# Three token groups cut anew (512, 64 + 768, 768), six PSUM banks for the first one's blocks, and moved steps in a one-core decoder layer

## The chip, the cores and the metric

The kernel runs on one core of one Trainium2 chip. The metric is the device time in microseconds of one execution. Before the change the median of three runs is 2630.23 us (2629.91 to 2632.38).

## What is computed

One layer of a decoder for 2048 prompt tokens and 64 sample tokens (8 sequences of 8), 1024 wide, in float32. Both kinds of token use the same weights; each sample sequence starts from a state of its own.

```python
def mixer(h, pos, s_ret, s_hg, w_in, ret_norm_w, hgrn_norm_w, lb, w_out):
    proj = h @ w_in                       # 1024 x 4096: rq rk rv rg hq hf hi hg, 4 heads of 128 each
    ...
    o_r, s_ret_new = chunk_gla(rq, rk, rv, log_g_ret, s_ret)     # retention, a fixed decay per head
    o_r = head_rmsnorm(o_r, ret_norm_w) * silu(rg)
    f = lb_h + (1.0 - lb_h) * sigmoid(hf)
    o_h, s_hg_new = chunk_gla(silu(hq) * dk ** -0.5, 1.0 - f, hi, log(f), s_hg)
    o_h = head_rmsnorm(o_h, hgrn_norm_w) * silu(hg)
    return concatenate([o_r, o_h]) @ w_out, s_ret_new, s_hg_new

x = x + mixer(rmsnorm(x, norm_mix_w), ...)
x = x + square(relu(rmsnorm(x, norm_ffn_w) @ w_up)) @ w_down     # 1024 x 4096, 4096 x 1024
y = rmsnorm(x, final_norm_w)
```

`chunk_gla` is the recurrence S_t = diag(g_t) S_(t-1) + k_t v_t^T, o_t = S_t^T q_t. Outputs are y for both kinds of token and the last states of both recurrences.

## The kernel before

**Groups.** Tokens lie along the free dimension, 128 features on the partitions. They are worked in three groups (`GROUPS`, L37): 64 sample + 512 prompt tokens, then 768, then 768 prompt tokens. Each group goes through the whole layer before the next; the recurrent states `S` are handed on. A group's slab is one tile of 128 x 768 float32 (`SLAB`, L29); the pool `sl` holds 46 (`NSLAB`), and `get` (L227) takes one. A group's columns are cut into two pieces for PSUM: twice 288 in the first group, twice 384 in the others (L391).

**Three products for one.** Every weight and activation is split into a high part in float32r (a cast on ScalarE) and the rest, the lower half (a subtraction on VectorE or GpSimd). A product is high x high, high x low and low x high, all float32r matmuls. `proj` (L314) runs a projection like that into a tile `pj` of two PSUM banks, of which there are two; four more banks form the pool `pm` (`mm`, L346), which the mixing and the norms use. `weight` (L242) casts weight tiles of 128 x 1024 two ahead of use; three of four lower halves (L271) are GpSimd's, the fourth VectorE's.

**Order.** The order of work is written out by hand. Each three-way step of a projection ends with a `tick` (L211), a count, not a time. Steps are put on an agenda with `at` and `later`, so many ticks on, and are issued when the count gets there; `flush` (L220) issues all that is left at once. A tick is two matmuls of a group's two pieces, or three matmuls in the values (`values`, L672). A scheduler orders the instructions of each engine by priority and free buffers after that; `keep_in_program_order` pins some.

**Stages of a group.** `norm_in` (L494) loads, casts and squares the group's input, spread over the end of the group before it, and turns its sum of squares into a factor per token. `mix` (L578) runs four heads; each projects its gates, keys, queries and values and puts the steps of `mixer` (L758) on the agenda: logs and scans, then for six block widths the exponents on GpSimd (L792), the exponentials on ScalarE (L797), the decayed products on VectorE (L803) and their matmuls (`level`); the products of a token with itself (`own`, summed over the partitions at L470, with halves cut at L331); the keys turned; then chunk by chunk the outputs (L997, L999) and states (L1005, with S on VectorE at L1012). A group with sample tokens also loads, uses and updates their states (L716 to L741). `out_proj_first` or `out_proj` (L1125, L1277) projects back: three heads' worth, added at L1119, then the fourth's, added at L1133 or L1292.

**FFN.** The first group's FFN is plain: 32 blocks up (`up_first`), 64 blocks down (`down_first`), each evicted by VectorE or ScalarE (L1198 is the addition after a down block). The other two use a seven-product scheme on 2 x 2 blocks (`up`, `down`, matmuls at L1105), apart from the first eighth of up. It needs sums of weight blocks. These are made during the first group's output projection and FFN: `plan_sums` (L1244) puts 15 sets on the agenda, each with four loads and four stores of 512 KB on the SP queue and four sums on VectorE (L1256), one set in 100 ticks from tick 90 after the mixing on.

**Last norm.** `finish_first` (L1213) and `finish` (L1578) normalize a group's result during the next group's mixing: eight squares on ScalarE, added on GpSimd (L491, L1588) every 8 ticks, then a sum over partitions, a factor (`last_factor`, L1623), and eight steps on VectorE (L1232, L1605) every 6 or 12 ticks, each followed by a store of y on SP. The last group ends with `finish(g, (1,), 1)` and `finish_last`.

Of the kernel before, what the change touches and what calls it, by code (L numbers as in the profile page):

```python
# [9 lines left out]
F32 = mybir.dt.float32  # L10
# [5 lines left out]
P = 128  # L16
# [12 lines left out]
SLAB = 768  # L29
NSLAB = 46  # L30
# [6 lines left out]
GROUPS = ((NS, 0, 512), (0, 512, 768), (0, 1280, 768))  # L37
# [58 lines left out]

def constants():
# [27 lines left out]
    pos = np.concatenate([np.tile(PAST + np.arange(SLEN), NSEQ), np.arange(SEQ)]).astype(np.float32)  # L125
# [72 lines left out]
class Kernel:  # L198
# [115 lines left out]
    def proj(self, g, blocks, acts, pieces=None):  # L314
# [3 lines left out]
        pj = self.pj.tile([P, 2, 512], F32, tag="pj", name="pj")  # L318
# [10 lines left out]
    def cut(self, src, hi, lo, T):  # L329
        self.tc.keep_in_program_order(self.nc.scalar.copy(hi[:, :T], src[:, :T]))  # L330
        self.nc.vector.tensor_tensor(out=lo[:, :T], in0=src[:, :T], in1=hi.bitcast(F32)[:, :T], op=ALU.subtract)  # L331

    def v2(self, slab, g):
        return slab[:, :g.T].rearrange("p (h t) -> p h t", h=2)
# [14 lines left out]
    def build(self):  # L349
        nc, tc, I = self.nc, self.tc, self.I  # L350
        with ExitStack() as ctx:
# [11 lines left out]
            self.ordered = True  # L363
# [21 lines left out]
            for ns, p0, n in GROUPS:  # L385
# [5 lines left out]
                g.pieces = [(0, g.T // 2), (g.T // 2, g.T)]  # L391
# [67 lines left out]
    def parts(self, src, n):  # L459

        t = self.getr()
        hi, lo = t[:, :n], t[:, SLAB // 2:SLAB // 2 + n]
# [9 lines left out]
    def halves(self, g, src):  # L472
        T2 = g.T // 2
        return [self.parts(src[:, hf * T2:(hf + 1) * T2], T2) for hf in range(2)]

    def both_sums(self, g, parts):

        out = []
        for hi, lo in parts:
            ps = self.mm(g.T // 2)  # L480
# [13 lines left out]
    def norm_in(self, g, start=False):  # L494


        nc, T, T2 = self.nc, g.T, g.T // 2
# [27 lines left out]
        def factor():  # L525
            g.rs, ln = self.get(), self.get()
            for hf in range(2):
                sl = slice(hf * T2, (hf + 1) * T2)
                ps = self.mm(T2)
# [46 lines left out]
        self.later(t0 + 28, factor_t, 3)  # L576
# [181 lines left out]
    def mixer(self, g, p, b, t0):  # L758
# [260 lines left out]
        step, late, chunk, wait = 13, 24, 7, 14  # L1019
# [4 lines left out]
        at(28, own, 0)  # L1024
        at(30, own, 1)
# [20 lines left out]
        at(t + 8, end_decays)  # L1046
# [687 lines left out]
```

## Time and profile before

| | |
|---|---|
| median of three runs | 2630.23 us |
| the profiled execution, its own time | 2629.84 us |
| its span, first to last instruction | 2628.0 us |
| ScalarE (ACT), busy | 1234.5 us (47%) |
| GpSimd (POOL), busy | 1089.9 us (41%) |
| mean granted TensorE clock | 0.995 |
| moved by DMA | 365.81 MB, 139 GB/s in the mean |

The first group's mixing is in the first 320 us of the span, its FFN ends near 795 us; the second group's mixing lies around 795 to 1210 us, the last one's FFN ends with the span.

The profile is one execution. PE is TensorE's matmuls, PEld its weight loads, which overlap them; DVE is VectorE, SP the engine that issues the transfers. A row of a group of instructions has line, engine, operation, output<-inputs, shapes and count; behind the bar the busy time and the mean ns of one, then the engine's idle time just before them and what ended it. A row of waits has who waited for whom, the total in us, how many times, and the longest. A matmul's mean is its latency; matmuls are pipelined, so the distance between two is shorter.

### The profile page before, as it was taken

To read this page: it belongs to the slowest core of one execution; us is meant where nothing else is said; L and a number is where in the kernel's file an instruction comes from. 1 tells how busy PE (TensorE), PEld (TensorE's weight loads), DVE (VectorE), ACT (ScalarE), POOL (GpSimd) and SP (SyncE) were. 2 spreads that over 40 slices of the span, in tenths; PEclk is the share of its full clock that TensorE was granted. 3 is DMA by queue.
4 is the path that set the end of the run, shared out by engine and by line. 5 is a ranking of instruction groups with operands and counts; after the bars stand their busy time and mean duration, and the time that the engine had idled before them with its cause. 6 is when DMAs were issued, how large, how long until landed. Compare 5 with 4: busy or idle time off the path is not lost. (4 is left out here: it accounts for less than half of the span.)

```text
span 2628.0 us, 41634 instructions
## 1 busy us (share of the span) xinstructions
PE 2570.6 (98%) x16999; PEld 2536.8 (97%) x16999; DVE 1683.9 (64%) x2077; ACT 1234.5 (47%) x1653; POOL 1089.9 (41%) x605
## 2 busy tenths in 40 slices
PE   8999999999999999999999999999999999999997
PEld 8999999999999999999999999989999999999997
DVE  6666776545565466565554988675665665549886
ACT  6555442222244555554543545455555445345443
POOL 6555557444436355431222332463554302223322
PEclk9999999999999999999999999999999999999999
DMA  5233366666752111122556755421111225566552
GB/s 181 81 97 90 121 217 241 232 252 221 266 183 85 57 49 49 53 66 69 166 174 203 261 169 199 145 97 49 46 44 59 70 69 178 179 207 209 175 178 81
DMA packets 125951, 365.81 MB, mean 139 GB/s; under 512 B 12480, under 2 KB 33984, under 8 KB 125760
## 3 DMA queue, kind: packets, MB, share of 16 engines
q1 hardware_dynamic: 125616, 363.13, 41.7%
q8 instruction: 134, 2.20, 0.3%
q14 instruction: 57, 0.47, 0.1%
q10 hardware_dynamic: 144, 0.02, 0.0%
HBM read 293.10 MB, written 69.99 MB: 138 GB/s over the span
## 5 line engine op out<-in xcount | busy, mean ns | idle before, releaser
L271 POOL TENSOR_TENSOR lo<-raw,hi 128x1024 fp32r<-128x1024 f32 x227 | 591.3, 2605 | 1257.6 <-ACT hi L256 1140.6
L323 PE MATMUL pj<-slab,hi 128*128 128x288 f32 (+1 forms) x5120 | 1016.8, 316 | 18.9 <-ACT hi L256 6.3
L323 PEld LDWEIGHTS pj<-slab,hi 128*128 128x128 f32 x5120 | 811.8, 189 | 25.2 <-ACT hi L256 9.3
L256 ACT CAST hi<-raw 128x1024 fp32r<-128x1024 f32 x402 | 422.3, 1052 | 847.1 <-PE pj L323 373.3
L323 PE MATMUL pj<-slab,lo 128*128 128x288 f32 (+1 forms) x2560 | 600.1, 315 | 1.8 <-POOL lo L271 1.7
L1105 PE MATMUL pd<-slab,hi 128*128 128x384 f32 x1792 | 457.2, 335 | 6.7 <-DVE slab L1551 3.1
L323 PEld LDWEIGHTS pj<-slab,lo 128*128 128x128 f32 x2560 | 430.0, 189 | 2.9 <-POOL lo L271 2.0
L1105 PE MATMUL pu<-slab,hi 128*128 128x384 f32 x1600 | 396.2, 334 | 0.0
L1105 PEld LDWEIGHTS pd<-slab,hi 128*128 128x128 f32 x1792 | 324.3, 188 | 8.4 <-DVE slab L1551 3.7
L271 DVE TENSOR_TENSOR lo<-raw,hi 128x1024 fp32r<-128x1024 f32 x175 | 231.6, 1323 | 156.0 <-ACT hi L256 152.7
L1105 PE MATMUL pd<-slab,lo 128*128 128x384 f32 x896 | 300.2, 335 | 0.9 <-POOL lo L271 0.9
L1105 PEld LDWEIGHTS pu<-slab,hi 128*128 128x128 f32 x1600 | 288.2, 188 | 0.0
L1105 PE MATMUL pu<-slab,lo 128*128 128x384 f32 x800 | 256.9, 334 | 0.0
L687 PE MATMUL pjv<-hi,slab 128*128 128x256 f32 x1088 | 211.6, 288 | 3.9 <-DVE slab L667 3.9
L1307 DVE TENSOR_TENSOR slab<-slab 128x768 fp32r<-128x768 f32 x144 | 162.3, 1143 | 41.4 <-ACT slab L1303 29.1
L687 PEld LDWEIGHTS pjv<-hi,slab 128*128 128x128 f32 x1088 | 175.5, 193 | 5.6 <-DVE slab L667 4.3
L1105 PEld LDWEIGHTS pd<-slab,lo 128*128 128x128 f32 x896 | 168.8, 188 | 1.5 <-POOL lo L271 1.5
L1303 ACT CAST slab<-slab 128x768 fp32r<-128x768 f32 x144 | 117.9, 833 | 108.3 <-DVE slab L1314 84.9
L687 PE MATMUL pjv<-lo,slab 128*128 128x256 f32 x544 | 155.0, 285 | 0.0
L1105 PEld LDWEIGHTS pu<-slab,lo 128*128 128x128 f32 x800 | 149.3, 188 | 0.0
L1521 DVE TENSOR_TENSOR slab<-pd,slab 128x768 f32<-128x768 f32 x110 | 104.1, 950 | 40.0 <-PE pd L1105 39.7
L797 ACT ACTIVATE slab<-slab 128x768 f32<-128x768 f32 (+2 forms) x72 | 56.3, 781 | 135.8 <-POOL slab L793 135.7
(197 smaller groups left out, 3405.2 us busy)
## 6 DMA issues: line engine op xcount, KB each, us to landing
raw<-w SPq DMA_DIRECT2D x342, 512.0 KB, 3.9
u<-ld SPq DMA_DIRECT2D x64, 384.0 KB, 4.6
slab<-u SPq DMA_DIRECT2D x64, 384.0 KB, 5.8
ld<-x SPq DMA_DIRECT2D x32, 384.0 KB, 4.6
y<-slab SPq DMA_DIRECT2D x12, 384.0 KB, 2.5
raw<-su1S SPq DMA_DIRECT2D x8, 512.0 KB, 3.7
raw<-su2S SPq DMA_DIRECT2D x8, 512.0 KB, 3.9
raw<-su3S SPq DMA_DIRECT2D x8, 512.0 KB, 4.0
```

Source lines behind the costliest of these rows:

```text
L256: self.nc.scalar.copy(hi, raw)
L271: eng.tensor_tensor(out=lo, in0=self.second.pop(j), in1=hi.bitcast(F32), op=ALU.subtract)
L323: self.nc.tensor.matmul(pj[:, i, :T2], w, a[:, c0:c1], start=j == 0 and q == 0, stop=j == n - 1 and q == 2)
L687: nc.tensor.matmul(pj[:, i * 256:(i + 1) * 256], a[:, s:s + C], ww, start=kb == 0 and q == 0, stop=kb == KB - 1 and q == 2)
L797: nc.scalar.activation(x["dd", w][:, a:T], x["dd", w][:, a:T], AF.Exp)
L1105: self.nc.tensor.matmul(*a, **k)
L1303: self.nc.scalar.copy(hi[:, :g.T], B[name][:, :g.T])
L1307: self.nc.vector.tensor_tensor(out=lo[:, :g.T], in0=B[name][:, :g.T], in1=hi.bitcast(F32)[:, :g.T], op=ALU.subtract)
L1521: nc.vector.tensor_tensor(out=r, in0=ps, in1=r, op=ALU.add)
```

## The change

What it does, by place:

- Groups are now 512 prompt tokens, 64 sample + 768 prompt tokens, 768 prompt tokens. The first group's columns are one piece of 512; the second's are two of 416. Slabs are 832 wide and 42 in number. Inputs, positions and outputs are laid out to match.
- From the first group's output projection to the end of its FFN (`spread`), two of three projections go to one bank of `pm`, the third to a `pj` tile.
- `plan_sums` runs ahead of the first mixing, one set in 148 ticks from tick 150 on.
- In `mixer`, the own sums come 4 ticks later, the exponentials and what follows them 2 ticks later; the second half of `cut` is issued 4 or 3 ticks after the first.
- In `out_proj_first` the lower halves come after 7 ticks instead of 4 and the flush at the end is gone; in `out_proj` they come 2 ticks later.
- The last norm's squares are added on VectorE, every 4 ticks; the output steps come every 5; the factor's last product is issued 4 ticks after what it needs. The last group's end keeps its pace and GpSimd.

```diff
-SLAB = 768
-NSLAB = 46
+SLAB = 832
+NSLAB = 42
...
-GROUPS = ((NS, 0, 512), (0, 512, 768), (0, 1280, 768))
+GROUPS = ((0, 0, 512), (NS, 512, 768), (0, 1280, 768))
...
         T2 = pieces[0][1] - pieces[0][0]
-        pj = self.pj.tile([P, 2, 512], F32, tag="pj", name="pj")
+        self.n_proj += 1
+        if self.spread and self.n_proj % 3:
+            pj = self.mm().unsqueeze(1)
+        else:
+            pj = self.pj.tile([P, 2, 512], F32, tag="pj", name="pj")
...
-    def cut(self, src, hi, lo, T):
+    def cut(self, src, hi, lo, T, lag=0):
         self.tc.keep_in_program_order(self.nc.scalar.copy(hi[:, :T], src[:, :T]))
-        self.nc.vector.tensor_tensor(out=lo[:, :T], in0=src[:, :T], in1=hi.bitcast(F32)[:, :T], op=ALU.subtract)
+        second = lambda: self.nc.vector.tensor_tensor(out=lo[:, :T], in0=src[:, :T], in1=hi.bitcast(F32)[:, :T], op=ALU.subtract)
+        self.later(lag, second) if lag else second()
...
-                g.pieces = [(0, g.T // 2), (g.T // 2, g.T)]
+                g.pieces = [(0, g.T)] if g.T <= 512 else [(0, g.T // 2), (g.T // 2, g.T)]
...
                 if i == 0:
+                    self.plan_sums(150, 148)
                     self.mix(g)
-                    self.plan_sums(90, 100)
+
+                    self.spread = True
                     self.out_proj_first(g)
                     self.ffn_first(g, nxt)
+                    self.spread = False
                     continue
...
-            self.cut(x["own"], x["own_hi"], x["own_lo"], T)
+            self.cut(x["own"], x["own_hi"], x["own_lo"], T, 4)
...
-            self.cut(x["quad"], x["quad_hi"], x["quad_lo"], T)
+            self.cut(x["quad"], x["quad_hi"], x["quad_lo"], T, 3)
...
-        step, late, chunk, wait = 13, 24, 7, 14
+        step, late, chunk, wait = 13, 26, 7, 14
...
-        at(28, own, 0)
-        at(30, own, 1)
+        at(32, own, 0)
+        at(34, own, 1)
...
             at(t, exponents, w)
-            at(t + 8, decays, w)
-            at(t + 11, decayed, w)
+            at(t + 10, decays, w)
+            at(t + 13, decayed, w)
             if w == 2:
-                at(t + 16, quad_products)
-                at(t + 20, quad_parts)
+                at(t + 18, quad_products)
+                at(t + 22, quad_parts)
...
-        at(t + 8, end_decays)
-        at(t + 12, tt, nc.vector, _Lazy(x, "kd"), _Lazy(x, "kd"), k)
-        at(t + 14, tt, nc.gpsimd, q, q, _Lazy(x, "eb"))
+        at(t + 10, end_decays)
+        at(t + 14, tt, nc.vector, _Lazy(x, "kd"), _Lazy(x, "kd"), k)
+        at(t + 16, tt, nc.gpsimd, q, q, _Lazy(x, "eb"))
         for sg in parts:
-            at(t + 27 + 3 * sg, turn, "kth", _Lazy(x, "kd"), sg, None)
-        t += 30
+            at(t + 29 + 3 * sg, turn, "kth", _Lazy(x, "kd"), sg, None)
+        t += 32
...
-            self.later(4, lambda acc=acc, hi=hi, lo=lo, wf=wf: nc.vector.scalar_tensor_tensor(
+            self.later(7, lambda acc=acc, hi=hi, lo=lo, wf=wf: nc.vector.scalar_tensor_tensor(
                 out=lo[:, :T], in0=acc[:, :T], scalar=wf, in1=hi.bitcast(F32)[:, :T], op0=ALU.mult, op1=ALU.subtract))
             h2[n] = (hi, lo)
-        self.flush()
...
-            x["sum"] = self.add_square(g, x["sum"], g.acc[n])
+            x["sum"] = self.add_square(g, x["sum"], g.acc[n], nc.vector)
...
-                self.last_factor(g, ps, r2[:, c0:c1], x["t"][:, c0:c1], c0, c1)
+                self.last_factor(g, ps, r2[:, c0:c1], x["t"][:, c0:c1], c0, c1, 4)
...
         for n in range(KB):
-            self.later(8 * n, square, n)
-            self.later(8 * KB + 26 + 6 * n, out, n)
-        self.later(8 * KB, split)
-        self.later(8 * KB + 10, factor)
+            self.later(4 * n, square, n)
+            self.later(4 * KB + 22 + 5 * n, out, n)
+        self.later(4 * KB, split)
+        self.later(4 * KB + 10, factor)
...
-                    self.later(6 + 6 * v + 6 * h, lo)
+                    self.later(8 + 6 * v + 6 * h, lo)
...
-                nc.gpsimd.tensor_tensor(out=x[h][:, :T], in0=x[h][:, :T], in1=t[:, :T], op=ALU.add)
+                (nc.gpsimd if per else nc.vector).tensor_tensor(out=x[h][:, :T], in0=x[h][:, :T], in1=t[:, :T], op=ALU.add)
...
-        pace, wait, gap, each = (3, 8, 6, 3) if per else (8, 10, 16, 12)
+        pace, wait, gap, each = (3, 8, 6, 3) if per else (4, 8, 10, 5)
...
-    def last_factor(self, g, ps, r2, t, c0, c1):
+    def last_factor(self, g, ps, r2, t, c0, c1, lag=0):
...
-        self.nc.vector.tensor_tensor(out=t, in0=t, in1=g.r[:, c0:c1], op=ALU.mult)
+        times = lambda: self.nc.vector.tensor_tensor(out=t, in0=t, in1=g.r[:, c0:c1], op=ALU.mult)
+        self.later(lag, times) if lag else times()
```

More of the change, by code (lines that the diff above doesn't have):

```diff
@@ L94, with in_groups @@
 NVEC = V_LB + 2 * H
+def in_groups(sample, prompt):
+    out = []
+    for ns, p0, n in GROUPS:
+        out += [sample[:ns], prompt[p0:p0 + n]]
+    return np.concatenate(out, 0)
 def constants():
@@ L362, in build @@
             self.raws, self.sums, self.side = {}, {}, deque()
-            self.ordered = True
+            self.ordered, self.spread, self.n_proj = True, False, 0
             self.ahead = 2
@@ L472, in halves @@
     def halves(self, g, src):
-        T2 = g.T // 2
-        return [self.parts(src[:, hf * T2:(hf + 1) * T2], T2) for hf in range(2)]
+        return [self.parts(src[:, c0:c1], c1 - c0) for c0, c1 in g.pieces]
     def both_sums(self, g, parts):
         out = []
-        for hi, lo in parts:
-            ps = self.mm(g.T // 2)
+        for (c0, c1), (hi, lo) in zip(g.pieces, parts):
+            ps = self.mm(c1 - c0)
             self.column_sums(ps, hi, lo)
@@ L526, in factor @@
             g.rs, ln = self.get(), self.get()
-            for hf in range(2):
-                sl = slice(hf * T2, (hf + 1) * T2)
-                ps = self.mm(T2)
+            for hf, (c0, c1) in enumerate(g.pieces):
+                sl = slice(c0, c1)
+                ps = self.mm(c1 - c0)
                 if start:
@@ L575, in norm_in @@
         self.later(t0 + 24, factor_t, 0)
-        self.later(t0 + 28, factor_t, 3)
+        for i in range(3, len(g.starts), 3):
+            self.later(t0 + 25 + i, factor_t, i)
     def mix(self, g):
@@ L1155, in mean @@
             x["q"] = self.get()
-            for hf, ps in enumerate(self.both_sums(g, x["parts"])):
-                nc.vector.tensor_scalar(out=x["q"][:, hf * T2:(hf + 1) * T2], in0=ps, scalar1=1.0 / D, scalar2=EPS,
+            for (c0, c1), ps in zip(g.pieces, self.both_sums(g, x["parts"])):
+                nc.vector.tensor_scalar(out=x["q"][:, c0:c1], in0=ps, scalar1=1.0 / D, scalar2=EPS,
                                         op0=ALU.mult, op1=ALU.add)
@@ L1593, in split @@
             x["parts", h] = self.pair_parts(g, x[h])
+            x["t", h] = self.get()
+            nc.scalar.activation(x["t", h][:, :T2], g.r[:, h * T2:(h + 1) * T2], AF.Square)
         def factor(h):
-            hc = slice(h * T2, (h + 1) * T2)
-            r2 = x["t", h] = self.get()
-            nc.scalar.activation(r2[:, :T2], g.r[:, hc], AF.Square)
-            self.last_factor(g, self.pair_sums(g, x["parts", h]), r2[:, :T2], r2[:, :T2], h * T2, (h + 1) * T2)
+            t = x["t", h][:, :T2]
+            self.last_factor(g, self.pair_sums(g, x["parts", h]), t, t, h * T2, (h + 1) * T2, 0 if per else 4)
         def out(np_, h):
```

23 lines of the change are left out of this document (12 added, 11 removed).

## The prediction

> **What bounds the kernel now.** I read the page's busy table and granted clock first, then stretches of the span, then TensorE's table of waits.
>
> ```profile
> span 2628.0 us, 41634 instructions
> PE 2570.6 (98%) x16999; PEld 2536.8 (97%) x16999; DVE 1683.9 (64%) x2077; ACT 1234.5 (47%) x1653; POOL 1089.9 (41%) x605
> PEclk9999999999999999999999999999999999999999
> ```
>
> TensorE (PE) is busy for 98% of the span and its clock is full in every slice. A time can fall only by what PE issues, or by the few waits between. Busy time counts overlapping matmuls once, so the price of a matmul is read from stretches in which PE issues one width without a gap (columns: stretch, length, then busy time and count of PE, PEld, DVE, ACT, POOL, then clock, DMA share, GB/s):
>
> ```profile
> 450.00:600.00 150.00, 150.00 (x1127) 150.00 (x1126) 74.93 (x64) 39.01 (x47) 67.17 (x30) 1.00 0.65 235
> 1096.50:1106.30 9.80, 9.80 (x84) 9.80 (x83) 7.30 (x9) 4.11 (x5) 7.21 (x4) 1.00 0.38 133
> 1300.00:1500.00 200.00, 200.00 (x1155) 200.00 (x1154) 126.72 (x123) 89.22 (x99) 56.83 (x21) 1.00 0.65 210
> ```
>
> The first is the first group's FFN, 288 columns per matmul. A count takes in the two matmuls cut by the edges, so 1125.5 start in 150 us: 133.3 ns each. The second, 256 columns, gives 9.8 / 82 = 119.5 ns. The third, 384 columns, gives 200 / 1153 = 173.5 ns. From 288 to 384 the slope is 40.2 / 96 = 0.4188 ns a column; carried back to 256 it gives 119.9, as measured. So a matmul costs **12.7 ns whatever its width, plus 0.4188 ns a column**.
>
> **The change, part by part.**
>
> *Groups of 512, 832, 768 and one piece in the first.* I count matmuls in the order of both built kernels; the first group's 288-wide projections can be checked here:
>
> ```profile
> L323 PE MATMUL pj<-slab,hi 128*128 128x288 f32 x3072 | 550.4, 300 | 14.2 <-ACT hi L256 6.3 <-DVE slab L1198 5.1 <-DVE slab L1133 2.8
> L323 PE MATMUL pj<-slab,lo 128*128 128x288 f32 x1536 | 334.9, 299 | 1.8 <-POOL lo L271 1.7
> ```
>
> These 4608 and 16 sums of squares become 2308 matmuls of 512 columns. No run here shows a 512-wide one of this type. The line gives 12.7 + 512 x 0.4188 = 227.1 ns; the ends are 214.4 (the fixed part gone) and 237 (288's price per column). I take 227.1, since three widths lie on that line. 416 columns cost 186.9, 320 cost 146.7, 448 cost 200.3. Before: 4624 of 288, 32 of 320, 8678 of 384, 1664 of 256. After: 2308 of 512, 4276 of 416, 32 of 448, 4370 of 384, 1704 of 256. Hence 524.1 + 799.2 + 6.4 + 40 x 119.8 = 1334.5 us added, and 616.4 + 4.7 + 4308 x 173.5 = 1368.5 us removed: **-34 us**. Some 29 are the 2316 fixed parts that go; the other 5 are columns, 64 tokens that now take the seven-product FFN. The rest of PE's work (the 128-wide products, the sample states) moves from the first group to the second, at the same count.
>
> The Trainium skill, "TensorE: Matmul & The Clock Gate", section "Back-to-back issue gap", puts a warm matmul at columns / 2.4 + 2.5 ns. The rows above are 11 ns above that at both widths, so they decide; by the page 512 columns would be 215.8 and the sum some 26 us lower.
>
> *First group's blocks in six banks, lower halves later.* From the output projection on, two blocks of three go to the four single banks, so PE may run five blocks ahead of VectorE instead of one. The waits this touches are in the two rows above (L1198, L1133) and here:
>
> ```profile
> 737.00:795.00 58.00, 53.44 (x371) 52.85 (x370) 36.61 (x38) 24.35 (x32) 21.94 (x12) 0.94 0.52 176
> ```
>
> Here the second group's input norm shares VectorE with the last FFN blocks. 371 matmuls at 133.3 ns need 49.5 us and take 58: 8.5 lost, 5.1 in waits and the rest to a clock of 0.94. With six banks VectorE may be five blocks late, 5 x 12 x 0.227 = 13.6 us. I take **-8**. What is late next is VectorE itself: its norm pieces are 832 wide instead of 768, over a shorter stretch. For L1133 (2.8 us) I take **-2.5**: the lower halves at seven ticks, and the flush dropped behind them, let the eviction pass first.
>
> *Mixing steps moved, last norm paced.*
>
> ```profile
> PE mm L470 <- DVE slab L331: 8.8, 9, 2.1
> PE pjv L687 <- DVE slab L667: 3.9, 2, 2.4
> 1746.00:1835.00 89.00, 85.52 (x567) 83.82 (x568) 55.92 (x91) 46.86 (x66) 39.43 (x25) 0.96 0.22 69
> L1232 DVE SCALAR_TENSOR_TENSOR slab<-slab,vec 128x576 f32<-128x576 f32 x8 | 11.3, 1479 | 0.0
> L604 DVE TENSOR_TENSOR slab<-pj,slab 128x768 f32<-128x768 f32 x2 | 1.9, 958 | 12.4 <-PE pj L323 12.4
> ```
>
> L470's nine waits are the sums over each head's own products, asked for 28 ticks into the head while VectorE still owes the lower half (L331). Four ticks more are twelve 256-wide matmuls, 1.4 us: more than all but the two of about 2 us. Those two, and L667's, stand at the head of groups two and three, where eight output steps (L1232, 11.3 us in one block of VectorE) precede L667. The new pace runs them 40 ticks earlier, where VectorE idles 12.4 us for PE (L604). The additions of squares that come from POOL to VectorE, seven and six, take about 1.4 us each there (next fence), some 10 us, and fit roughly that idle time. Behind each output step SP issues a y store, ahead of weight loads; both go earlier together. Waits of 12.7 us and a clock of 0.96 over 89 us (3.6) make 16.3; I take **-15**. If VectorE were not idle there, the same 15 would stay.
>
> *Weight sums from the first mixing on, mixing in shorter ticks.* Fifteen sets of four VectorE sums, four loads and four stores spread over 148 ticks each instead of 100; four or five sets now fall into the first group's mixing.
>
> ```profile
> L491 DVE TENSOR_TENSOR slab<-slab 128x576 f32<-128x576 f32 x3 | 4.1, 1361 | 0.6 <-ACT slab L488 0.5
> L1256 DVE TENSOR_TENSOR raw<-raw 128x1024 f32<-128x1024 f32 x60 | 103.4, 1723 | 0.8 <-issue 0.2
> 66.00:141.00 75.00, 74.70 (x585) 71.73 (x584) 49.48 (x90) 41.93 (x70) 42.01 (x36) 1.00 0.27 85
> 320.00:420.00 100.00, 95.38 (x717) 94.23 (x716) 77.46 (x70) 39.56 (x61) 58.31 (x27) 1.00 0.60 198
> L719 PE MATMUL po<-slab,ld 128*128 128x128 f32 x128 | 15.6, 275 | 0.0
> L733 PE MATMUL mm<-slab 128*128 128x512 f32 x32 | 15.0, 592 | 0.0
> L730 DVE TENSOR_TENSOR slab<-slab,con 128x512 f32<-128x512 f32 x4 | 3.0, 800 | 0.0
> L740 DVE TENSOR_TENSOR ld<-ld,mm 128x512 f32<-128x512 f32 x2 | 1.4, 688 | 2.2 <-POOL ld L739 2.0 <-PE mm L733 0.2
> L737 DVE SCALAR_TENSOR_TENSOR ld<-ld,mm 128x512 f32<-128x512 f32 x2 | 1.4, 682 | 1.0 <-PE mm L733 1.0
> ```
>
> One head of the first group is 75 us, PE busy for 74.7 of it, VectorE for 49.5 (66%). Of the 75, 288 matmuls of 288 columns are 38.4, 120 of 256 are 14.4, the sample states (L719, L733) 30.6 / 4 = 7.7, the rest 14.5. After: 144 x 0.227 = 32.7, 96 x 0.1198 = 11.5, no samples, 14.5: 58.7 us. VectorE keeps (49.5 - 5.8) x 512 / 576 = 38.8, less some smaller sample steps, and gets 4 x 1.72 a set; a set is 148 of the head's 176 ticks, so 8.2 a head. That makes 47 of 58.7, **80% busy**. No row shows the mixing at that load. The two ends are 66:141 (0.3 lost in 75) and 320:420, the nearest in load (77% VectorE, 4.6 lost in 100). Over 235 us that is 1 to 11 us; I take **+7**, nearer the second. The stores wait on SP for VectorE, ahead of the weight loads, but weights are asked for two ahead (some 10 us), and DMA is at 0.27 of its time here against 0.65 in the FFN. If that cover fails, it falls under the same 11. In the FFN VectorE is half idle already (74.9 of 150), so giving sums up there gains nothing. L271's wait (1.7 us) at the start of the FFN grows with ticks 15% shorter: **+1**.
>
> *Wider slabs, 42 for 46.* In the order of both kernels the pool is full only in the down products, and after the change also at the end of the second group's mixing. I take 0, up to +5. The end of the kernel keeps its steps: 0. The later lower half at L1307: 0, its wait is VectorE's evictions.
>
> **Sum**, against the profiled execution's 2629.84 us (0.4 below the median 2630.23): -34 - 8 - 2.5 - 15 + 7 + 1 = -51.5, so **2578 us**.
>
> **The rivals.**
>
> *A head of the first group doesn't get shorter (slower).* If the chain POOL exponents, ACT exponentials, VectorE products, not PE, sets a head once its ticks shrink, the head stays at 75 us and the sums add their 8.2: 83 against 58.7, four times: 97 - 7 more, 2668. If only the 75 stay, 4 x 16.3 - 7 = 58 more, 2636. It decides when VectorE's work and its waits pass 58.7 us a head. For: 80%, with products that wait on two engines. Against: 49.5 us of work in 75, hardly a wait. 7% (5% full, 2% the weaker form).
>
> *A wide matmul is no cheaper per column.* 231 (384's price per column) to 237 ns: 9 to 23 more, 2587 to 2601. Three widths speak against. 7%.
>
> *The waits stay.* The moved steps meet the norm's and the gates' own work, and 8 + 15 come back: 2601. 11%.
>
> *The fixed part goes at 512 columns*, because a stream that long covers it: 2308 x 12.7 = 29 less, 2549. Constant from 256 to 384 speaks against. 6%.
>
> *PE loses clock while it cycles through six banks.* At 0.94, as in 737:795, the FFN's 1536 x 0.227 = 349 us lose 22: 2600. Here the low clock followed waits of 2.8 us, and 450:600 holds 1.00. 3%. The Trainium skill, same page, section "A second HAM failure mode: psum-queue depth-cycling", reports such an oscillation for 512-wide matmuls that cycle through banks; no run here shows it yet.
>
> **How the numbers follow.** The forecast has 66%. Its own range is 2560 to 2596 (6 us of waits, 12 of the mixing). The 80% range takes in the wide matmul, the waits and the clock, and most of the other price end: **2550 to 2612**. Outside are the slower rival, most of the 2549 case and some tail. A measurement of this kernel tells 0.2%, 5 us, from no change: faster 93%, within 2%, slower 5%.
>
> **What would show it.** Stretches of pure 512-wide matmuls: 227 ns apiece is right, over 231 wrong. A head of the first group should take 59 to 62 us with VectorE near 80%; 70 or more is the slower rival. L1198, L331 and L667 should be under 3 us together in TensorE's waits, the clock 1.00 at both group changes. It is wrong if S (L1012) or the decayed products (L804) head TensorE's waits with over 15 us.

## The result and the profile after

Four runs of the changed kernel have a median of 2656.59 us (2649.91 to 2658.52), four of the kernel before 2631.31 us. The ratio is 1.0092, 95% interval [1.0074, 1.0109]: **slower by 25 us, where some 52 fewer were predicted**. The profiled executions, 2658.52 and 2629.84 us, differ by 28.7. Line numbers are those of the changed kernel from here on; L485/L486 are what L469/L470 were, L343 was L331, L946 was L930, L853 was L837, L819/L820 were L803/L804, L813 was L797.

The page of the changed kernel, its first lines:

```profile
span 2656.5 us, 37153 instructions
PE 2568.3 (97%) x14689; PEld 2424.2 (91%) x14689; DVE 1766.8 (67%) x2086; ACT 1240.0 (47%) x1647; POOL 1055.9 (40%) x592
```

2310 matmuls fewer, and yet 28.5 us more of span. Two stretches that hold matmuls of one width without a gap, the first group's FFN (512 columns) and the second group's (416), in the columns of the same view of before:

```profile
450.00:600.00 150.00, 150.00 (x664) 124.20 (x663) 74.70 (x65) 45.35 (x58) 76.52 (x36) 1.00 0.62 224
1300.00:1500.00 200.00, 200.00 (x1060) 198.14 (x1059) 128.46 (x111) 83.41 (x89) 52.22 (x19) 1.00 0.58 197
```

150 / 662.5 = 226.4 ns and 200 / 1058.5 = 188.9 ns: as predicted at 512 columns, 2 ns more than predicted at 416. So most of the time is lost between matmuls. TensorE's table of waits, first rows:

```profile
PE mm L946 <- DVE AT L853: 25.4, 8, 3.6
PE pj L335 <- ACT hi L264: 6.2, 1, 6.2
PE mm L749 <- DVE slab L746: 5.7, 3, 1.9
PE pj L335 <- ACT slab L713: 4.7, 3, 2.2
PE mm L486 <- DVE slab L343: 4.4, 4, 2.9
```

The wait that headed the table before (8.8 us, nine times) has shrunk to 4.4, and of that only 0.2 lies behind 690 us. In its place stands a new one, 25.4 us in eight waits. L946 is `ret_scores`, which needs a bank of the pool `mm`; L853 is VectorE's copy of the results of `own`, which frees one. The other stretch that changed is the first mixing. Stretches of the changed kernel (the first 300 us, with the first mixing; then the mixing of the second and of the third group):

```profile
0.00:300.00 300.00, 270.66 (x1567) 228.12 (x1568) 223.96 (x358) 184.33 (x299) 163.67 (x127) 0.98 0.44 158
690.00:1190.00 500.00, 477.83 (x3041) 458.82 (x3040) 300.92 (x431) 217.68 (x303) 216.28 (x145) 0.97 0.20 66
1755.00:2150.00 395.00, 381.75 (x2592) 375.49 (x2591) 241.06 (x362) 194.63 (x275) 175.87 (x106) 0.98 0.17 57
```

and of the kernel before:

```profile
0.00:300.00 300.00, 289.32 (x2246) 278.25 (x2247) 202.54 (x351) 176.99 (x283) 174.29 (x153) 1.00 0.34 107
690.00:1190.00 500.00, 489.47 (x3396) 482.69 (x3395) 290.07 (x425) 246.65 (x344) 235.64 (x135) 0.99 0.27 90
1755.00:2150.00 395.00, 390.46 (x2646) 384.12 (x2646) 241.54 (x377) 208.09 (x300) 165.28 (x100) 1.00 0.18 55
```

In each of the three TensorE idles 9 to 19 us more, and its clock is 0.02 lower. The stages lie a little apart in the two kernels.

To compare kernels whose stages don't lie at the same times I use one measure below, the **loss**: each distance from one matmul's start to the next, less the distance that its width has where nothing hinders it (227.5 ns at 512 columns, 188.6 at 416, 173.6 at 384, 133.3 at 288, 119.75 at 256, 110.8 for the short float32 products of 128, 429 for the 32 plain float32 products of 512 on the sample tokens' states), summed over a stretch. It is good to a microsecond. It holds waits and low clock together. The rest of the span is TensorE's own work, 2533.6 us before and 2506.7 after, and about 17 us ahead of the first and behind the last matmul. The loss is 76.8 us before and 132.4 after: **-27 of work, +55.6 of loss**, which makes the 28.5 us of span up to half a microsecond. Of the 55.6, 32.8 are in the first 300 us (11.5 before, 44.3 after), 22.8 behind them.

### The profile page after: what moved, and what is told of

Read it like the earlier page. It is cut to its first block, busy times and chain, and to the rows that moved or that the text cites. A ratio compares the mean times of both kernels' runs of the same rounds, so it can differ in the third digit from the quotient of the medians.

```text
span 2656.5 us, 37153 instructions
## 1 busy us (share of the span) xinstructions
PE 2568.3 (97%) x14689; PEld 2424.2 (91%) x14689; DVE 1766.8 (67%) x2086; ACT 1240.0 (47%) x1647; POOL 1055.9 (40%) x592
## 5 line engine op out<-in xcount | busy, mean ns | idle before, releaser
L335 PE MATMUL pj<-slab,hi 128*128 128x416 f32 (+2 forms) x2844 | 748.6, 366 | 10.9 <-ACT hi L264 6.2
L335 PEld LDWEIGHTS pj<-slab,hi 128*128 128x128 f32 x2844 | 514.9, 190 | 44.1 <-ACT hi L264 6.2
L1121 PE MATMUL pd<-slab,hi 128*128 128x416 f32 (+1 forms) x1792 | 469.4, 342 | 5.1 <-DVE slab L1566 3.1
L335 PE MATMUL pj<-slab,lo 128*128 128x416 f32 (+2 forms) x1422 | 437.1, 365 | 2.2 <-POOL lo L279 2.0
L1121 PE MATMUL pu<-slab,hi 128*128 128x416 f32 (+1 forms) x1600 | 408.2, 342 | 0.0
L1121 PE MATMUL pd<-slab,lo 128*128 128x416 f32 (+1 forms) x896 | 307.8, 344 | 0.0
L335 PEld LDWEIGHTS pj<-slab,lo 128*128 128x128 f32 x1422 | 260.8, 189 | 19.8 <-POOL lo L279 2.5
L1121 PE MATMUL pu<-slab,lo 128*128 128x416 f32 (+1 forms) x800 | 264.2, 343 | 0.0
L335 PE MATMUL mm<-slab,hi 128*128 128x512 f32 x740 | 231.2, 392 | 2.2 <-DVE slab L1152 2.2
L703 PE MATMUL pjv<-hi,slab 128*128 128x256 f32 x1088 | 218.2, 294 | 2.8 <-ACT hi L264 1.4
L1322 DVE TENSOR_TENSOR slab<-slab 128x832 fp32r<-128x832 f32 (+1 forms) x144 | 163.0, 1149 | 36.8 <-ACT slab L1318 17.5
L703 PEld LDWEIGHTS pjv<-hi,slab 128*128 128x128 f32 x1088 | 181.6, 200 | 4.6 <-DVE slab L683 1.6
L703 PE MATMUL pjv<-lo,slab 128*128 128x256 f32 x544 | 158.4, 291 | 2.0 <-POOL lo L279 2.0
```

Of the source, the lines that this page charges most:

```text
L335: self.nc.tensor.matmul(pj[:, i, :T2], w, a[:, c0:c1], start=j == 0 and q == 0, stop=j == n - 1 and q == 2)
L703: nc.tensor.matmul(pj[:, i * 256:(i + 1) * 256], a[:, s:s + C], ww, start=kb == 0 and q == 0, stop=kb == KB - 1 and q == 2)
L1121: self.nc.tensor.matmul(*a, **k)
L1322: self.nc.vector.tensor_tensor(out=lo[:, :g.T], in0=B[name][:, :g.T], in1=hi.bitcast(F32)[:, :g.T], op=ALU.subtract)
```

## Experiments: the copy that holds the banks

The theory after the comparison: `own`, four ticks later, is no longer copied out ahead of VectorE's next decayed products but behind them, and its two banks stay taken. The rival: the loss is the first mixing's alone, and the table of waits shows only where it comes to light.

**Own early again.** The changed kernel with one edit undone; the lag of 4 ticks in the split of the own products stays:

```diff
-        at(32, own, 0)
-        at(34, own, 1)
+        at(28, own, 0)
+        at(30, own, 1)
```

> The changed kernel with the sums over each head's own products back at 28 and 30 ticks (32 and 34 after the change); all else as changed. Theory A: the four later ticks put VectorE's copy out of these sums (L853) behind the decayed products of the third block width, so the PSUM banks of the sums stay taken and the retention scores (L946) wait: here the copy stands ahead of those products again, L946's 25.4 us of waits fall under 4, the clock returns to about 0.990, L343 gets back up to 9 us, and the time is 2622 to 2635. Rival: the banks are late because the second group is wider or slabs are fewer; then L946 still waits for 20 us or more and the time stays within 5 us of 2656.

Measured: 2634.62 us, ratio to before 1.0013 [1.0004, 1.0022], 22 us under the changed kernel. The first theory held:

```profile
PE mm L486 <- DVE slab L343: 12.3, 11, 2.9
PE mm L946 <- DVE AT L853: 1.8, 2, 0.9
```

So the 25.4 us in the table and the clock behind them are worth 22 us net of what comes back.

**Own late in the kernel before,** and nothing else:

```diff
-        at(28, own, 0)
-        at(30, own, 1)
+        at(32, own, 0)
+        at(34, own, 1)
```

> The kernel before, with one edit: the sums over a head's own products at 32 and 34 ticks in place of 28 and 30. Theory A (the later ticks alone put VectorE's copy L837 behind the decayed products of the third width): L930, the retention scores, waits about 3 us in each of the eight heads of groups two and three, 20 to 26 us in all, the clock falls to about 0.99 behind these waits, L331's 8.8 us go, and the time is 15 to 30 us over before. Rival (the wait needs the wide second group or fewer slabs too): L930 waits under 5 us, and the time is 3 to 9 us under before for L331's waits.

Measured: 2655.55 us (2654.29 to 2656.35), ratio 1.0096 [1.0081, 1.0111]. The first theory held. That these two edited numbers alone give the size of the whole slowdown is chance: in the changed kernel other gains and losses, of about equal sums, stand beside them. TensorE's first row of waits (lines as in the kernel before):

```profile
PE mm L930 <- DVE AT L837: 22.0, 8, 4.0
```

How two edited numbers do that is seen in VectorE's instructions, in order of time. The kernel before, second group, second head:

```profile
934.80 1.23 DVE L804 TENSOR_TENSOR slab<-slab 128x384 f32<-128x384 f32 x1
935.96 1.18 DVE L464 TENSOR_TENSOR slab<-slab 128x384 fp32r<-128x384 f32 x1
937.06 1.05 DVE L837 COPY_PREDICATED AT<-msk,mm 128x384 f32<-128x384 uint8 x2
938.01 0.53 DVE L803 TENSOR_TENSOR slab<-slab 128x384 f32<-128x384 f32 x1
```

The same head with own at 32 and 34 in the kernel before:

```profile
934.24 1.23 DVE L804 TENSOR_TENSOR slab<-slab 128x384 f32<-128x384 f32 x1
935.39 1.18 DVE L464 TENSOR_TENSOR slab<-slab 128x384 fp32r<-128x384 f32 x1
936.50 1.25 DVE L803 TENSOR_TENSOR slab<-slab 128x384 f32<-128x384 f32 x1
937.67 0.55 DVE L804 TENSOR_TENSOR slab<-slab 128x384 f32<-128x384 f32 x1
938.14 1.04 DVE L837 COPY_PREDICATED AT<-msk,mm 128x384 f32<-128x384 uint8 x2
```

The copy L837 has fallen behind L803 and L804 of the next width. And the changed kernel, where the same pair and a second copy for the sample tokens stand ahead of it (VectorE, then TensorE):

```profile
852.05 1.21 DVE L480 TENSOR_TENSOR slab<-slab 128x416 fp32r<-128x416 f32 x1
853.19 1.25 DVE L819 TENSOR_TENSOR slab<-slab 128x384 f32<-128x384 f32 x1
854.37 0.54 DVE L820 TENSOR_TENSOR slab<-slab 128x384 f32<-128x384 f32 x1
854.83 0.21 DVE L852 COPY_PREDICATED ATs<-msk,mm 128x64 f32<-128x64 uint8 x1
854.97 1.03 DVE L853 COPY_PREDICATED AT<-msk,mm 128x384 f32<-128x384 uint8 x2
```

```profile
844.75 0.37 PE L485 MATMUL mm<-slab,ones_r 128*128 128x448 f32 x1
...
845.88 0.34 PE L485 MATMUL mm<-slab,ones_r 128*128 128x384 f32 x1
...
848.84 0.56 PE L889 MATMUL mm<-slab 128*64 128x64 f32 x6
...
850.60 0.56 PE L889 MATMUL mm<-slab 128*64 128x64 f32 x6
...
855.68 1.62 PE L946 MATMUL mm<-slab 128*128 128x128 f32 x6 [3.61 <-DVE AT L853]
```

TensorE has the sums (L485) done at 846 us. They hold two of the four banks until the copies at 855; the corners of width 64 (L889) take the other two at 849 and 851; L946 finds none and waits 3.61 us.

**What a wait costs beside itself.** Granted clock in the 6 us behind five of these eight waits (they end at 742.7, 855.7, 1081.7, 1780.3 and 2059.2 us and lasted 3.37, 3.61, 3.61, 3.45 and 2.31 us):

```profile
742.70:748.70 6.00, 5.99 (x27) 5.97 (x28) 1.97 (x5) 1.73 (x5) 0.00 (x0) 0.50 0.00 1
855.70:861.70 6.00, 6.00 (x28) 5.97 (x29) 1.97 (x6) 1.76 (x5) 0.00 (x0) 0.53 0.01 3
861.70:867.70 6.00, 6.00 (x59) 5.45 (x58) 4.22 (x5) 3.26 (x7) 4.17 (x2) 1.00 0.13 33
1081.70:1087.70 6.00, 5.98 (x31) 5.97 (x32) 1.97 (x6) 1.79 (x5) 0.00 (x0) 0.59 0.01 3
1780.30:1786.30 6.00, 6.00 (x25) 6.00 (x26) 4.04 (x7) 4.35 (x8) 0.29 (x1) 0.50 0.27 90
2059.20:2065.20 6.00, 5.99 (x31) 5.99 (x32) 3.80 (x7) 4.58 (x9) 0.97 (x1) 0.72 0.25 87
```

After the six microseconds it is at 1.00 again (third row). Over all eight waits the missing clock is (0.50 + 0.47 + 0.46 + 0.41 + 0.50 + 3 x 0.28) x 6 = 19 us, nearly as much as the 25.4 us of waiting: so by this estimate a wait of 3 us costs 5 to 6. The waits that these replaced were eight of 0.7 to 2.1 us. In the kernel with all the old ticks (below), the clock is 1.00 in the 6 us behind L946's two waits of 0.9 us. The Trainium skill, "TensorE: Matmul & The Clock Gate", section "HAM oscillation — how this bites in real kernels", lets the clock fall to half after gaps of more than some 3.4 us; the direction agrees, but here waits of 2.31 to 2.95 us were enough.

**The scores later.** If L946 alone is asked for too early, moving it ends the wait; if banks are short, the next user of a bank gets it. In the changed kernel (the scores of the sample tokens then come behind the scaling of their queries, a changed part of the computation, here and in the run with own and the scores late):

```diff
-            at(46 + 4 * sg, ret_scores, sg)
+            at(54 + 4 * sg, ret_scores, sg)
```

> The changed kernel, with the retention scores asked for at 54 ticks instead of 46; own sums stay at 32 and 34. Theory A, by way of the banks: four single banks are taken by the two own sums and the two corners of width 64, so the fifth user waits for the first copy; asked for 8 ticks later (some 3 us) L946 waits under 6 us and nothing takes its place, and the time is 2615 to 2635. Rival: the next user of a bank (the sums of next products, or the corners of width 32) inherits the wait, 15 us or more under another line, and the time stays over 2645.

Measured: 2645.51 us, ratio 1.0057 [1.0042, 1.0072]. The row that now heads the table:

```profile
PE mm L485 <- DVE AT L853: 13.5, 8, 2.2
```

Still eight waits, still for L853: it is the bank, not the scores. The expectation had this as its rival (with 15 us or more, and over 2645 us); its first theory, that nothing takes the wait's place, was wrong.

**All of the mixing's steps at their old ticks.** The changed kernel with the two cuts' lags, `late`, own, decays, decayed, quad and the end of the head as before:

```diff
-        step, late, chunk, wait = 13, 26, 7, 14
+        step, late, chunk, wait = 13, 24, 7, 14
-        at(32, own, 0)
-        at(34, own, 1)
+        at(28, own, 0)
+        at(30, own, 1)
-            at(t + 10, decays, w)
-            at(t + 13, decayed, w)
+            at(t + 8, decays, w)
+            at(t + 11, decayed, w)
...
-        t += 32
+        t += 30
```

> The changed kernel with every step of the mixing at its old tick (own sums, exponentials, decayed products, turned keys, cuts without a lag). Theory A: as in the run with the own sums alone, and the other moves are worth little: within 6 us of it. Rival: the later exponentials and products pay for themselves in the first group's short ticks; then this run is 10 us or more above the one with the own sums alone, and the first 300 us lose more than the 44 us that they lose in the changed kernel.

Measured: **2616.75 us** (2615.82 to 2617.43), ratio 0.9945 [0.9931, 0.996]: faster than the changed kernel and the kernel before. From the first run of this section it differs by the other moved steps, which thus cost 18 us by themselves; neither theory had that. Of the 18, 5 lie in the first 300 us (loss 47.3 there, 42.3 here). The table of waits shows of them L749's 5.7 us and 4.5 us of L764 for L876, both gone here, and L486's for L343, 12.3 there, where the split still lags, and 7.9 here.

**Own and the scores late, the rest at the old ticks.**

> The changed kernel with old ticks in the mixing, apart from own sums at 32 and 34 and retention scores at 54. Beside the run with all old ticks (2617) it should lose L343's 7.9 us of waits without getting L946's. Theory A by way of the banks: 2606 to 2615. Rival (a later bank user inherits): 2620 or more.

Measured: 2631.87 us (2627.91 to 2637.29), ratio 1.0006 [0.9997, 1.0015]. L485 waits for L853 eight times, 10.5 us: the rival again. Both moves together are 15 us worse than neither.

**The split of the own products earlier,** in the best kernel found so far (next section, sums from tick 400):

```diff
-        at(12, own_parts)
+        at(8, own_parts)
```

> The kernel of 2609.64 us with the split of each head's own products at tick 8 and not 12, so that the sums over them at ticks 28 and 30 find their lower half done without holding banks for longer. Theory A (L486's nine waits for L343, 8.9 us there, are a matter of when the subtraction is asked for): under 3 us in those waits, 2599 to 2606 us. Theory B (VectorE has other work ahead of it whenever it is asked for): 6 us or more stay, 2607 to 2614 us.

Measured: 2608.88 us against 2609.64 without the edit, and the wait stays:

```profile
PE mm L486 <- DVE slab L343: 9.6, 10, 1.6
```

The second theory held. In the second group's third head, in both runs, the cast (L342) ends 3.3 us before the wait does, and the subtraction L343 starts 1.6 us behind the cast, after VectorE's L685. So there it is VectorE's order, not the tick of the request.

## Experiments: the first mixing

**Sums late again,** in the changed kernel:

```diff
-                    self.plan_sums(150, 148)
                     self.mix(g)
+                    self.plan_sums(90, 100)
```

> The changed kernel with the weight sums planned after the first mixing, one set in 100 ticks, as before the change. Theory B: the sums, 1.7 us each on VectorE, make TensorE wait in the first mixing: what is lost in the first 300 us falls from 44 to about 20 us, the time to 2630 to 2640, with L946's 25 us of waits unchanged. Rival: the waits there come from ticks that are 20% shorter in time while VectorE's, GpSimd's and ScalarE's steps are not; then the first 300 us lose 35 us or more and the time stays above 2646.

Measured: 2660.98 us, ratio 1.0115 [1.01, 1.013]. The first 300 us lose 28.9 instead of 44.3, but behind them the FFN more than pays it back: in 300 to 690 us TensorE is busy for 368.94 of 390, where it was 382.98. Neither theory gave both.

**Groups and slabs as before,** everything else as in the changed kernel, without the six banks:

```diff
-GROUPS = ((0, 0, 512), (NS, 512, 768), (0, 1280, 768))
+GROUPS = ((NS, 0, 512), (0, 512, 768), (0, 1280, 768))
-                    self.spread = True
+                    self.spread = False
```

> The changed kernel with the groups of before (64 + 512, 768, 768 tokens, two pieces of 288, 46 slabs of 768) and so without the six banks, which need one piece; the moved steps, the paced last norm and the early sums stay. If the forecast's price of the matmuls holds, TensorE's own work rises by 34 to 36 us. Theory C (short ticks make the first mixing wait): that mixing's loss falls from 44 to 20 us or less, L946 still waits 20 us or more in groups two and three, and the time is 2655 to 2675. Rival (sums and own sums alone make the waits): the first mixing still loses 35 us or more and the time is 2680 or more.

Measured: 2655.6 us, ratio 1.0092 [1.0075, 1.0109], loss of the first 300 us 25.6, 19 less than with the new groups; the first theory in time and kind, though it had 20 us or less. L946 waits for L853 here too: 19.7 us in eight.

**The sums from the first mixing on, alone,** in the kernel before:

```diff
-                    self.mix(g)
-                    self.plan_sums(90, 100)
+                    self.plan_sums(150, 148)
+                    self.mix(g)
```

> The kernel before with its weight sums planned as in the changed kernel, from the first mixing on, and nothing else. Theory A (the sums cost some 14 us in any first mixing, by the other runs): the loss of the first 300 us goes from 11.5 to 20 to 28 us, the loss of 300 to 750 us falls by less, 2632 to 2644 us. Theory B (at 576 columns a head is long enough to hide them, and only the new groups make them cost): the first 300 us lose under 15 us, 2624 to 2632 us.

Measured: 2638.85 us, ratio 1.0036 [1.0022, 1.0049]; loss of the first 300 us 22.5, that is 11 more than before: the first theory. One stretch of the first mixing in this kernel:

```profile
115.00:178.00 63.00, 60.73 (x475) 57.74 (x474) 49.02 (x77) 33.72 (x52) 40.36 (x33) 1.00 0.44 149
```

and in the kernel before:

```profile
115.00:178.00 63.00, 63.00 (x495) 60.24 (x494) 42.61 (x78) 33.19 (x52) 37.37 (x33) 1.00 0.30 93
```

With VectorE at 78% instead of 68% TensorE idles 2.3 us of 63, where it didn't idle at all.

**The new groups, one piece and slabs alone,** in the kernel before.

> The kernel before with the new groups, slabs and the one piece of 512 alone: no six banks, no paced last norm, old mixing steps, weight sums after the mixing. TensorE's own work is 36 us less. Theory C: the shorter ticks cost the first mixing some 15 us (its first 300 us lose about 27 against 12 before), the waits of before on L331, L667 and the FFN's down blocks remain; 2605 to 2622. Rival: the first mixing's loss belongs to the early sums only; then its first 300 us lose under 16 us and the time is 2590 to 2604.

Measured: 2642.9 us, ratio 1.0048 [1.0031, 1.0064]. Neither theory: the loss is that of the first one and more, the time lies above both ranges. Of the work that goes (27 us by the prices above, not the 36 expected) nothing is left over. The first 300 us lose 30.8, 19 more than before, with VectorE no busier (198.57 us, 202.54 before); and the first group's down blocks wait for banks (L1214 here is L1213 elsewhere):

```profile
PE pj L335 <- DVE slab L1214: 14.3, 9, 3.0
PE mm L486 <- DVE slab L343: 11.7, 9, 3.5
```

The 300 us hold the start of the output projection here (from 264 us on, where it was 308 before). Of the 19, some 6 lie ahead of the first head's mixing, in the first 57 us. TensorE comes to the weights of the first values (L703) at 36 us and waits for their casts twice within 4 us; its clock falls behind that. The waits, and the stretch here and in the kernel before:

```profile
PE pjv L703 <- POOL lo L279: 2.0, 1, 2.0
PE pjv L703 <- ACT hi L264: 1.5, 1, 1.5
0.00:57.00 57.00, 46.07 (x231) 38.52 (x232) 38.67 (x55) 36.69 (x54) 33.04 (x35) 0.94 0.54 192
0.00:57.00 57.00, 48.49 (x360) 47.03 (x361) 39.70 (x56) 38.51 (x56) 35.23 (x35) 1.00 0.57 190
```

The kernel before has neither wait; the changed kernel has both. Some 3 more are waits of about 1 us, one at the start of each of the other three heads, for ScalarE's copies of the values (L713).

**The same in two pieces of 256 columns:**

```diff
-                g.pieces = [(0, g.T)] if g.T <= 512 else [(0, g.T // 2), (g.T // 2, g.T)]
+                g.pieces = [(0, g.T // 2), (g.T // 2, g.T)]
```

> The kernel before with the new groups and slabs, the first group in two pieces of 256 columns and not in one of 512 (the run with the new groups alone had one piece: 2642.9 us, 31 us lost in the first 300). TensorE's own work grows by 4616 x 119.75 less 2308 x 227.5 ns, some 28 us. Theory A (one piece is what costs in the first mixing: whoever waits for a result waits for all 512 columns, and a block has no second half to go on with): the loss of the first 300 us falls to 10 to 17 us, and the waits for L1214 go too: 2636 to 2656 us. Theory B (it is the shorter ticks or the other cut of the groups): 26 to 33 us lost there, 2662 to 2674 us.

Measured: 2658.89 us, ratio 1.011 [1.0094, 1.0125]. TensorE's own work is some 28 us more; the first 300 us lose 22.9, and time and loss both lie between what the two theories gave. So the single piece is 8 of the 19 us, and the waits for L1214 hardly depend on it (12.8 us, eight times). The other 11 are not its doing: the waits for weights at the start and for L713 are here too (3.2 and 3.0 us).

**The first group's steps later.** The kernel with the old mixing steps, with every step of the first group's mixing at 11/10 of its tick:

```diff
-        at = lambda t, fn, *a: self.at(t0 + t, fn, *a)
+        at = lambda t, fn, *a: self.at(t0 + (t * 11 // 10 if T <= 512 else t), fn, *a)
...
-        return t0 + t + 10
+        return t0 + ((t + 10) * 11 // 10 if T <= 512 else t + 10)
```

> The changed kernel with every mixing step at its old tick (as in the run with the old mixing steps, 2616.75 us), and the first group's mixing steps at 11/10 of those ticks, so that 67 is followed by the work that stood one tenth later. Theory A (in the first mixing the loss comes from ticks that are shorter, 512 rows a matmul and not 576, while the vector work of a step is nearly the same, so that a step is issued before its inputs are ready): the loss of the first 300 us, 42 us in that run, falls to 30 or less, and the time to 2600 to 2610. Theory B (the loss there is the sum of work of VectorE and of the weight sums that share it, wherever the steps stand): the loss stays at 38 to 46 us and the time at 2612 to 2621.

Measured: 2624.16 us, ratio 0.9977 [0.9968, 0.9986]; the first 300 us lose 50 instead of 42. Neither theory: worse. A tenth more time for the steps does not help, which speaks against steps that are issued too early in shorter ticks.

**The sums begun later.** The kernel with the old mixing steps, then:

```diff
-                    self.plan_sums(150, 148)
+                    self.plan_sums(400, 134)
```

> The changed kernel with every mixing step at its old tick, and the weight sums planned at a third of the rate in the first mixing (the rest after it). Theory A (the sums' vector work in the first mixing costs about 14 us there and can be hidden when it is spread thinner): loss of the first 300 us 42 to about 32 us, nothing given back later, 2605 to 2610 us. Theory B (what is not done there is done later beside other full stretches of VectorE, as with all sums after the first mixing): the loss of the first 300 us falls by 5 to 14 us, that of 300 to 750 us grows by as much, 2612 to 2622 us.

The expectation describes the edit wrongly: the sums begin 250 ticks later, at nearly the old rate. 13 of the 60 fall into the first 300 us, not 18. Measured: **2609.64 us** (2609.12 to 2609.94), ratio 0.9921 [0.9906, 0.9936]; the first 300 us lose 33.5 instead of 42.3, and little comes back later. With a start at tick 600, 120 apart:

> The kernel with every mixing step at its old tick and the sums begun at tick 600 and 120 apart (400 and 134 gave 2609.64 us). Theory A (each set that leaves the first mixing gains more there than it costs behind it): 2602 to 2608 us, the first 300 us lose 30 us or less. Theory B (the best split is at hand already): 2608 to 2616 us, what the first 300 us gain is lost in 300 to 750 us.

Measured: 2616.4 us, ratio 0.9949 [0.9932, 0.9966]; the first 300 us lose 32.8, hardly less, and from 300 to 900 us 26.7 instead of 19.1. That is the second theory, at the end of its range.

## Experiments: six banks and the last norm

**No six banks** in the kernel with the old mixing steps:

```diff
-                    self.spread = True
+                    self.spread = False
```

> The changed kernel with every mixing step at its old tick, and the first group's down blocks in the old banks, not in six. Theory A (the last down block of the first group waits for banks that the copies out hold, as the nine waits of L1214 did in the kernel before with the new groups alone, 14.3 us): 2628 to 2640 us, with those waits on L1213 or L1214. Theory B (the six banks are worth nothing, or cost clock): 2605 to 2619 us.

Measured: 2634.62 us, ratio 1.0016 [1.0007, 1.0026], 18 us over the kernel with six: the first theory. The new head of the table:

```profile
PE pj L335 <- DVE slab L1213: 14.4, 9, 3.4
```

The new groups need the six banks: 5.1 us of this wait before had become 14.4. What the prediction named from the Trainium skill, "TensorE: Matmul & The Clock Gate", section "A second HAM failure mode: psum-queue depth-cycling", did not show here: with six banks the clock is 1.00 over 450 to 600 us (row above), and without them the kernel is slower.

**The last norm as before** (not paced, its squares on GpSimd), in the kernel with the old mixing steps:

```diff
-            x["sum"] = self.add_square(g, x["sum"], g.acc[n], nc.vector)
+            x["sum"] = self.add_square(g, x["sum"], g.acc[n])
-            self.later(4 * n, square, n)
+            self.later(8 * n, square, n)
...
```

> The changed kernel with every mixing step at its old tick, and the last norm as it was before: not paced, its squares on GpSimd. Theory A (the paced norm is what took the waits of L667 and L683 at the group changes away): those waits and L343's at the heads of groups 2 and 3 come back, 6 to 15 us, so 2623 to 2632 us. Theory B (the norm stands beside work that hides it either way): within 4 us of 2616.75.

Measured: 2625.09 us, ratio 0.9978 [0.9968, 0.9987], 8 us over the paced one. The first theory by its size; the waits show 4.5 of the 8, at L683 (2.5 us against 1.3) and L343 (11.2 against 7.9).

## Why the prediction was wrong

**Right but for 7 us: TensorE's work.** -34 predicted, some -27 measured; 227.1 ns predicted at 512 columns, 226.4 and 227.5 measured. The two rivals on that price fall. For 416 columns 186.9 ns were predicted, measured 188.6 to 188.9: up to 2 ns on 4276 matmuls, which is the 7 us.

**Right in kind, too small: six banks (-10.5).** L1198's and L1133's waits are gone, but TensorE now waits 2.2 us in two waits for the lower halves themselves (L1152), which come at seven ticks: of the -2.5 little is left. The worth of the banks in the kernel with the new groups is 18 us, since the groups would have made L1198's waits worse.

**Wrong: "Four ticks more are twelve 256-wide matmuls, 1.4 us: more than all but the two of about 2 us."** This is the step that failed, by 25 us, and with it the -15 of which it is part. Its first half came true: behind 690 us, L486 waits 0.2 us for L343. But it priced the moved step only by the wait that it leaves, not by what it is moved past. `own` ends in a copy on VectorE that frees two banks; four ticks on, that copy stands behind the decayed products of the next width, and `ret_scores` waits 2.3 to 3.6 us for a bank, eight times, with a clock of 0.50 to 0.72 behind each wait. Alone it costs 24 to 25 us (2655.55 against the kernel before). The prediction came near with the products L804 as a place to watch, yet as one that TensorE would wait for, not as what stands ahead of the copy. The other moved steps of the mixing, put at nothing without a reason, cost 18. The paced norm, the other part of the -15, did bring 8.

**Wrong in size, by as much: the first mixing (+7).** VectorE's load was right: 47 of 58.7 us predicted, 45 to 48 us of 58 to 63 measured. Its price was not: 32.8 us measured, where the bounds were 1 and 11. The sums alone are 11 of it (in the kernel before), the upper bound. The bounds left out the groups themselves, 19 us. 8 go with the single piece of 512; that it is finished only as a whole is the theory's reason, and only the size was measured. Some 5 are waits for the casts of weights at the start and the clock behind them: the prediction's cover, weights asked for two ahead, fails there, with the sums early or late. Some 3 are the waits for L713, and the rest is open. Why TensorE now comes too soon is open as well: a tenth more time for the mixing's steps did not help, and that the sample tokens' products, which left this group, had filled such gaps would fit, but wasn't tried.

**The sum.** Work -27; the first 300 us +33; own +25; the other steps +13 (5 of their 18 are in the first 300 us already); L1198's and L1133's waits, the low clock there and L1152's new wait some -9; the norm -8: +27, measured +25 (medians) and +28.7 (profiled executions). Each is from another kernel, so this checks sizes and nothing finer. Of the rivals, the one that ended slower (a first head that doesn't get shorter) gave a time near the measured one (2636 to 2668 us) for another reason. That is luck: the heads take 58 to 63 us, about as forecast.

## What to carry to other kernels

Before a step is moved by a few ticks, list what it moves past on every engine that it uses, its last instruction above all: the one that frees a buffer. A wait that is taken away at 1 us apiece may come back at 3, at the next user of the buffer that is now held longer. When a piece of work is made larger to save fixed cost, look for what used the seams between the pieces.

## What the runs showed of the hardware

- A TensorE wait of 2.3 to 3.6 us was followed by a granted clock of 0.50 to 0.72 over the next 6 us, in all eight waits of L946; behind waits of 0.9 us it stayed at 1.00. With own late in the kernel before it was seven of eight: one wait of 2.67 us was followed by 1.00. In the run with the scores later, three waits of 2.18 us were followed by 1.00, 0.72 and 0.72. So near 2 us the length of a wait alone does not decide it here.
- In the trace's record of the clock each fall is to 0.50, in the changed kernel for 3.41 or 6.83 us: 0.72 over 6 us is half speed for 3.4 of them.
- The float32r matmuls' distance goes on almost linearly to a whole bank: 119.75, 173.6, 188.6 and 227.5 ns at 256, 384, 416 and 512 columns; only 416 lies off the line, by 1.5 ns.
